# A gated merge of two token mixers: its steps in written order, four weights fetched early, three output tiles in program order

## The chip, the cores and the metric

The kernel runs on one core of a Trainium2 chip. The metric is device microseconds (us) of one execution, the median of several runs. Within the core, TensorE (PE) multiplies, VectorE (DVE) and ScalarE (ACT) work elementwise, GpSimd (POOL) does small sums and issues some transfers, and SyncE (SP) issues most transfers. Every engine works through its own queue in order.

## The reference, cut to what matters

One layer of an encoder block on x of 512 rows by 1024 columns, all in float32:

```
x = x + 1/2 * SwiGLU(RMSNorm(x))                       # FFN 1
h = RMSNorm(x); p = h @ W_in                           # all projections of the mixers and gates
y_A = RWKV7(...) @ rwkv_proj                           # 8 heads x 64
y_B = ForgettingAttention(...) @ fox_proj              # 8 heads x 64
x = x + (sigmoid(g_A) * y_A + sigmoid(g_B) * y_B) @ w_out      # the merge
x = x + 1/2 * SwiGLU(RMSNorm(x))                       # FFN 2
out = RMSNorm(x)

# the end of RWKV7, per head of 64 columns:
y = (y - mean(y)) * rsqrt(var(y) + eps) * lnx_g + lnx_b
y = (y + bonus) * (sigmoid(g_lo) @ g_up)
```

## The kernel before

Activations lie transposed: a tile is 128 columns of the model (partitions) by the 512 rows of x. A product in float32 is made of three fast matmuls: every operand is split into a high part and a low part (`hi` is a rounded copy made on ScalarE, `lo` the difference made on VectorE), and hi x hi, hi x lo and lo x hi are summed in one PSUM bank (`mm3`).

A weight tile goes this way: SP issues its transfer into a `raw` buffer (three of them, in rotation, so a transfer waits until VectorE has made the low half of the tile three before), ScalarE makes `whi`, VectorE `wlo` (two pairs, in rotation, so a cast waits until TensorE has read the pair two before). `own=` gives a split weight a buffer of its own instead: with a number n, the tiles in which the normed inputs `xh{n}` and `xl{n}` stand at other times.

The stage of the change is the merge. Before it stand the delta rule of RWKV-7 (in chunks), the attention, and the last gates (`early`, PSUM tile `pgt`). The merge itself has these parts:

- `proj` with `fox_proj`: eight output tiles (m = 0 to 7, called fox 0 to fox 7 here) of twelve matmuls each into the bank `ppj`; the gate step on VectorE (`G<-G,ppj`) empties the bank.
- The norm of RWKV's output for four head pairs p: `center` times y gives the centred y in the bank `yc` (two matmuls, y being split into `parts`); ScalarE squares it; the square is split (`shi`, `slo`) and summed over the head by two matmuls into the bank `pg`; ScalarE takes logarithm and exponential (`Tall`); VectorE multiplies, scales and adds the bonus; one product in full float32 with `gup` (written as two TensorE records per matmul) gives the gate, VectorE multiplies by it, and the result is split into `ya`.
- `proj` with `rwkv_proj`: eight tiles of twelve matmuls (rwkv 0 to 7), which need all four `ya`; VectorE adds the two mixers, and the sum is split (`mh`, `ml`). Three of the gates' tanhs (`late_tanh`) stand on ScalarE behind the last `ya`, after a table load.
- `w_out`: eight tiles of 24 matmuls into the bank `pw`; VectorE adds the residual, and the norm for FFN 2 begins.

The program is written in one order, and a scheduler of the framework places the instructions on each engine's queue by a simulated time. Two tools override it: `tc.issue_after(x)`, which places what is under it behind x, and `tc.keep_in_program_order(x)`, by which x keeps its place in the written order of its engine. In the merge of the kernel before, only table loads are kept; matmuls of the norm, of fox_proj, of rwkv_proj and of w_out are placed by the scheduler, which lets tiles run into each other.

Of the kernel before, what the change touches and what calls it, by code (L numbers as in the profile page):

```python
# [12 lines left out]
AF = mybir.ActivationFunctionType  # L13
ALU = mybir.AluOpType
# [4 lines left out]
P = 128  # L19
T = 512  # L20
D = 1024
KD = D // P
# [3 lines left out]
NP = DA // P  # L26
# [9 lines left out]
PAR_W0, PAR_A0, PAR_KK, PAR_KA, PAR_RK, PAR_LG, PAR_LB = 38, 42, 46, 50, 54, 58, 62  # L36
# [15 lines left out]
def kernel(  # L52
# [6 lines left out]
    nc = tc.nc  # L59
    dve, act, pool, pe = nc.vector, nc.scalar, nc.gpsimd, nc.tensor  # L60
# [37 lines left out]
    epsl = cp.tile([P, 1], F32, name="epsl")  # L98
# [4 lines left out]
    sel = cp.tile([P, 8], F32, name="sel")  # L103


    def load_raw(aps, kt, n, raw=None):
        if raw is None:
            raw = wp.tile([P, kt, n], F32, tag="raw", name="raw", bufs=3)
        for c0, src in aps:
            nc.sync.dma_start(raw[:, :, c0:c0 + src.shape[1]],  # L110
                              src.rearrange("(k p) c -> p k c", p=P))
        return raw

    def split_w(raw, kt, n, eng=None, own=None):
        if own is None:
            hi = wp.tile([P, kt, n], F32R, tag="whi", name="whi", bufs=2)
            lo = wp.tile([P, kt, n], F32R, tag="wlo", name="wlo", bufs=2)
        elif isinstance(own, int):
            hi, lo = [xp.tile([P, kt, n], F32R, tag=f"x{i}{own}", name=f"own{i}{own}") for i in "hl"]
        else:  # L120
            hi, lo = own
        act.copy(hi[:], raw[:])  # L122
        (eng or dve).tensor_tensor(lo[:], raw[:], hi[:].bitcast(F32), op=ALU.subtract)  # L123
        return hi, lo

    def load_w(aps, kt, n, eng=None, own=None):
        return split_w(load_raw(aps, kt, n), kt, n, eng, own)

    def mm3(ps, whi, wlo, xhi, xlo, first, last):
        pe.matmul(ps, whi, xhi, start=first, stop=False)  # L130
        pe.matmul(ps, whi, xlo, start=False, stop=False)  # L131
        return pe.matmul(ps, wlo, xhi, start=False, stop=last)  # L132

    def ln_act(out, in_, **kw):
        pre = act.preload_act_table_set("natural_log_exp_and_others")
# [4 lines left out]
    def halved(src):  # L140
        hi, lo = tmp("shi", dt=F32R), tmp("slo", dt=F32R)
        act.copy(hi[:], src)
        dve.tensor_tensor(lo[:], src, hi[:].bitcast(F32), op=ALU.subtract)
        return hi, lo

    def summed(ps, mat, parts):
        for i, part in enumerate(parts):
            pe.matmul(ps, mat[:], part[:], start=i == 0, stop=i == 1)

    def exact(ps, mat, src):  # L150
        summed(ps, mat, halved(src))

    def split(dst_hi, dst_lo, src, hi_eng="act"):
        cast = act.copy(dst_hi, src) if hi_eng == "act" else dve.tensor_copy(dst_hi, src)
        dve.tensor_tensor(dst_lo, src, dst_hi.bitcast(F32), op=ALU.subtract)
        return cast
# [77 lines left out]
    def pc(i):  # L234
        return par[:, i:i + 1]
# [11 lines left out]
    with tc.tile_pool(name="x0", bufs=1) as x0:  # L247
        xin = [x0.tile([P, NB, D // 4], F32, name=f"xin{g}") for g in range(4)]
        own = [[x0.tile([P, KD, P], F32R, name=f"first{i}{w}") for i in "hl"] for w in range(2)]
        wraw = [x0.tile([P, KD, P], F32, name=f"wraw{w}") for w in range(2)]  # L250
        first = []
# [5 lines left out]
        for c in range(KD):  # L257
            ps = bank("xtp", pr)
# [79 lines left out]
    def ffn(nrm, w1, w3, w2, nxt, during=(), first=None, final=None):  # L338
        with tc.tile_pool(name="hp", bufs=1) as hp:
# [86 lines left out]
    with ExitStack() as mx:  # L426
# [7 lines left out]
        def duo(tag, name, dt=F32):  # L434
            return sp.tile([P, 2, T], dt, name=name, tag=tag)
# [33 lines left out]
        lg = tmp("lg")  # L469
# [44 lines left out]
        vs = [V4[:, p] for p in range(NP)]  # L514
# [141 lines left out]
        for t in range(C - 1):  # L656
            n, m = t + 1, C - 1 - t
# [177 lines left out]
        for p in range(NP):  # L835
# [16 lines left out]
            for i, bl in enumerate(((0, 1), (2,), (3,))):  # L852
                at = {b: sum(c + 1 for c in bl[:j]) * P for j, b in enumerate(bl)}
                w = sum(b + 1 for b in bl) * P
                lps, trs = [], []
                for q in range(2):
                    lp = pf.tile([P, T], F32, tag="b", name="lp")
                    lps.append(lp)
                    for b in bl:
                        n, bs = (b + 1) * P, slice(b * P, (b + 1) * P)  # L860
# [4 lines left out]
                for q in range(2):  # L865
                    pt, mx = pts[:, q], mx_[q]
                    for b in bl:
                        n, mb = (b + 1) * P, mx[:, b:b + 1]
# [29 lines left out]
                    early(3 * p - 2 + i)  # L898
            yb.append(qp)

        def proj(m, wt, y):
            wh, wl = load_w([(0, wt[0][:, m * P:(m + 1) * P])], NP, P)
            ps = bank("ppj")
            for k in range(NP):
                mm3(ps[:], wh[:, k, :], wl[:, k, :], y[k][0], y[k][1], k == 0, k == NP - 1)
            return ps


        def halves(tiles):
# [19 lines left out]
        for p in range(NP):  # L929
            y = vs[p]  # L930
            yc = bank("yc", pr)
            for i in range(2):
                pe.matmul(yc[:], center[:], parts[p][i], start=i == 0, stop=i == 1)
            sq = gslot[8 + p % 2]
            act.activation(sq, yc[:], AF.Square)
            ps = bank("pg", pf)
            exact(ps[:], bonesr, sq)
            rn = tslot[p]
            with tc.issue_after(logs.ins):
                act.activation(rn, ps[:], AF.Ln, bias=epsl[:, 0:1], scale=1.0 / 64)  # L940
                act.activation(rn, rn, AF.Exp, scale=-0.5)
            dve.tensor_tensor(y, yc[:], rn, op=ALU.mult)
            dve.scalar_tensor_tensor(y, y, pc(PAR_LG + p), bons[p], op0=ALU.mult, op1=ALU.add)
            ps = bank("pg", pf)
            pe.matmul(ps[:], gup[0:96, p * P:(p + 1) * P], lg[0:96, :], start=True, stop=True)
            dve.tensor_tensor(y, y, ps[:], op=ALU.mult)
            parted = split(*ya[p], y)
# [7 lines left out]
        for m in range(KD):  # L955
            g = gslot[m]
            nc.gpsimd.dma_start(g, gsave[KD + m])
            ps = proj(m, fox_proj, ybs)
            dve.scalar_tensor_tensor(g, g, 1.0, ps[:], op0=ALU.add, op1=ALU.mult)
        fctx.close()  # L960


# [6 lines left out]
        def late_tanh(m, behind):  # L969
            if m < NP + 3:  # L970
                with tc.issue_after(behind.ins):
                    act.activation(slot[m], slot[m], AF.Tanh, scale=0.5)
# [7 lines left out]
        ms = []  # L980
# [90 lines left out]
```

## Time and profile before

| | us |
|---|---|
| median of 3 runs | 1191.12 (1190.68 to 1191.21) |
| profiled execution | 1190.24 |
| its span in the profile | 1188.5 |
| TensorE busy | 1169.2 (98%) |
| VectorE busy | 662.1 (56%) |
| ScalarE busy | 457.1 (38%) |
| first fox_proj matmul to first matmul of FFN 2 | 715.85 to 815.51 |

The profiled execution is one run; its span is 1.7 us shorter than its own time, and its time is 0.9 us under the median. In the rows of the profile "L130" is a line of the kernel, "out<-in" names tiles, "x2" counts instructions, and in brackets stands the idle time of the engine just before, and what ended it.

### The profile page before, as it was taken

What the parts mean: (1) busy time and instruction counts of PE and PEld (TensorE: products, weight loads), DVE (VectorE), ACT (ScalarE), POOL (GpSimd) and SP (SyncE); (2) the same over time, 40 slices, a digit from 0 to 9 for tenths busy, and PEclk for the clock granted to TensorE, in tenths of its full rate; (3) what the DMA queues carried; (4) which work ended last, traced back from release to release, by engine and by line L of the source; (5) the groups of instructions that cost most, each with busy time, mean ns of one, the idle gap of its engine ahead of it and who ended that gap; (6) DMA issues with size and microseconds to landing.
All of it is one profiled execution on the core that took longest, in us unless ns stands there. A gap on an engine that the chain in (4) does not pass through costs nothing.

```text
span 1188.5 us, 15870 instructions
## 1 busy us (share of the span) xinstructions
PE 1169.2 (98%) x6334; PEld 952.3 (80%) x6334; DVE 662.1 (56%) x993; ACT 457.1 (38%) x739; POOL 100.4 (8%) x144
## 2 busy tenths in 40 slices
PE   8999999999999999999999999999999999999997
PEld 7888888888887888887767777778888888888887
DVE  6555545443444888686766657866545545543242
ACT  6322222222223855346776756524222222222221
POOL 4200000001111112401000011121000000000110
PEclk9999999999999999999999999999999999999999
DMA  7333333323333433344212135633333333323331
GB/s 200 89 91 104 89 106 89 103 83 115 116 116 96 121 108 111 111 124 116 55 46 87 55 99 175 193 100 107 89 98 98 90 105 91 104 80 98 98 98 72
DMA packets 208152, 122.54 MB, mean 103 GB/s; under 512 B 9902, under 2 KB 200430, under 8 KB 208078
## 3 DMA queue, kind: packets, MB, share of 16 engines
q1 hardware_dynamic: 202078, 108.67, 31.8%
q0 software_dynamic: 3760, 12.06, 3.2%
q8 instruction: 50, 0.82, 0.3%
q10 hardware_dynamic: 2240, 0.79, 0.3%
q14 instruction: 24, 0.20, 0.1%
HBM read 110.82 MB, written 10.68 MB: 102 GB/s over the span
## 4 chain that ended last, share of the span: by engine, by line
PE 95%; DVE 3%; ACT 1%; DMA 1%; issue 0%; POOL 0%; SPq 0%; DVEq 0%; POOLq 0%
PE pd L131 7%; PE pd L130 7%; PE pd L132 7%; PE pa L132 7%; PE pa L131 7%; PE pb L131 7%; PE pb L132 7%; PE pa L130 7%; PE pb L130 7%; PE pgt L130 3%; PE pgt L132 2%; PE pgt L131 2%; PE pk L130 2%; PE pk L132 2%; PE pk L131 2%; PE pw L132 1%
## 5 line engine op out<-in xcount | busy, mean ns | idle before, releaser
L122 ACT CAST whi<-raw 128x1024 fp32r<-128x1024 f32 (+2 forms) x197 | 196.4, 998 | 605.9 <-PE pa L131 175.5
L123 DVE TENSOR_TENSOR wlo<-raw,whi 128x1024 fp32r<-128x1024 f32 (+2 forms) x197 | 227.5, 1155 | 129.1 <-ACT whi L122 129.0
L132 PE MATMUL pa<-xh,wlo 128*128 128x512 f32 x344 | 133.9, 389 | 0.0
L131 PE MATMUL pa<-xl,whi 128*128 128x512 f32 x344 | 133.8, 389 | 0.0
L132 PE MATMUL pb<-xh,wlo 128*128 128x512 f32 x344 | 133.8, 389 | 0.0
L130 PE MATMUL pa<-xh,whi 128*128 128x512 f32 x344 | 133.8, 389 | 0.0
L130 PE MATMUL pb<-xh,whi 128*128 128x512 f32 x344 | 133.8, 389 | 0.0
L131 PE MATMUL pb<-xl,whi 128*128 128x512 f32 x344 | 133.8, 389 | 0.0
L132 PE MATMUL pd<-hh,wlo 128*128 128x512 f32 x330 | 129.0, 391 | 0.0
L131 PE MATMUL pd<-hl,whi 128*128 128x512 f32 x330 | 128.5, 389 | 0.0
L130 PE MATMUL pd<-hh,whi 128*128 128x512 f32 x330 | 128.4, 389 | 0.0
L350 DVE TENSOR_TENSOR fb<-pb,rstd 128x512 f32<-128x512 f32 x43 | 29.7, 691 | 137.2 <-PE pb L132 137.2
L130 PEld LDWEIGHTS pa<-xh,whi 128*128 128x128 f32 x344 | 64.6, 188 | 13.5
L132 PEld LDWEIGHTS pb<-xh,wlo 128*128 128x128 f32 x344 | 64.6, 188 | 13.4
L131 PEld LDWEIGHTS pb<-xl,whi 128*128 128x128 f32 x344 | 64.6, 188 | 13.5
L132 PEld LDWEIGHTS pa<-xh,wlo 128*128 128x128 f32 x344 | 64.5, 188 | 13.5
L131 PEld LDWEIGHTS pa<-xl,whi 128*128 128x128 f32 x344 | 64.6, 188 | 13.4
L130 PEld LDWEIGHTS pb<-xh,whi 128*128 128x128 f32 x344 | 64.5, 188 | 13.4
L131 PEld LDWEIGHTS pd<-hl,whi 128*128 128x128 f32 x330 | 61.9, 188 | 12.9
L132 PEld LDWEIGHTS pd<-hh,wlo 128*128 128x128 f32 x330 | 62.0, 188 | 12.7
L130 PEld LDWEIGHTS pd<-hh,whi 128*128 128x128 f32 x330 | 62.0, 188 | 12.7
L346 DVE TENSOR_TENSOR fa<-pa,rstd 128x512 f32<-128x512 f32 x43 | 29.7, 691 | 68.5 <-PE pa L132 68.4
(397 smaller groups left out, 1964.5 us busy)
## 6 DMA issues: line engine op xcount, KB each, us to landing
raw<-in_ffn_w_dram SPq DMA_DIRECT2D x116, 512.0 KB
raw<-in_w_in_dram SPq DMA_DIRECT2D x40, 512.0 KB
raw<-in_ffn_w_dram SPq DMA_DIRECT2D x15, 384.0 KB
raw<-in_w_out_dram SPq DMA_DIRECT2D x8, 512.0 KB
gsave<-gs SPq DMA_DIRECT2D x9, 256.0 KB
xin<-in_x_dram SPq DMA_DIRECT2D x4, 512.0 KB
xsave<-xT POOLq DMA_DIRECT2D x8, 256.0 KB, 2.3
G<-gsave POOLq DMA_DIRECT2D x8, 256.0 KB, 3.8
```

The lines of the kernel that those rows point to most:

```text
L122: act.copy(hi[:], raw[:])
L123: (eng or dve).tensor_tensor(lo[:], raw[:], hi[:].bitcast(F32), op=ALU.subtract)
L130: pe.matmul(ps, whi, xhi, start=first, stop=False)
L131: pe.matmul(ps, whi, xlo, start=False, stop=False)
L132: return pe.matmul(ps, wlo, xhi, start=False, stop=last)
L346: dve.tensor_tensor(a[:], pa[:], nrm.rstd[:], op=ALU.mult)
L350: dve.tensor_tensor(b[:], pb[:], nrm.rstd[:], op=ALU.mult)
```

## The change

The products of fox_proj and the steps of the norm are written in an explicit order (`fox`, `centred`, `squared`, `summing`, `normed_y`), and their matmuls keep it on TensorE. The first four rwkv_proj weights (`ahead_of`, m = 0 to 3) are fetched and split between fox_proj's tiles 4 to 7, each into a buffer of its own. The transfers of the fox weights from m = 4 on and of all rwkv weights keep their written order on SP. In w_out the matmuls of the first three tiles keep the written order. The number of instructions of each kind and their shapes stay the same.

```diff
-    def load_raw(aps, kt, n, raw=None):
+    def load_raw(aps, kt, n, raw=None, keep=False):
...
+            if keep:
+                tc.keep_in_program_order(got)
...
-    def mm3(ps, whi, wlo, xhi, xlo, first, last):
...
+    def mm3(ps, whi, wlo, xhi, xlo, first, last, keep=False):
+        for n, (w, x_) in enumerate(((whi, xhi), (whi, xlo), (wlo, xhi))):
+            mm = pe.matmul(ps, w, x_, start=first and n == 0, stop=last and n == 2)
+            if keep:
+                tc.keep_in_program_order(mm)
+        return mm
...
-        def proj(m, wt, y):
-            wh, wl = load_w([(0, wt[0][:, m * P:(m + 1) * P])], NP, P)
+        def proj_w(m, wt, own=None):
+            return load_w([(0, wt[0][:, m * P:(m + 1) * P])], NP, P, own=own, keep=wt is rwkv_proj or m > 3)
+
+        def proj(w, y):
+            wh, wl = w
             ps = bank("ppj")
             for k in range(NP):
-                mm3(ps[:], wh[:, k, :], wl[:, k, :], y[k][0], y[k][1], k == 0, k == NP - 1)
+                for n, (a, b) in enumerate(((wh, 0), (wh, 1), (wl, 0))):
+                    keep(pe.matmul(ps[:], a[:, k, :], y[k][b], start=k == 0 and n == 0, stop=k == NP - 1 and n == 2))
             return ps
...
+        fox(0)
+        for p in range(NP):
+            centred(p, pr if p < 3 else pf)
+        squared(0)
+        squared(1)
+        fox(1)
+        squared(2)
+        squared(3)
+        fox(2)
+        summing(0)
+        summing(1)
+        fox(3)
+        summing(2)
+        summing(3)
+        rw = []
+
+        def ahead_of(m):
+            rw.append(proj_w(m, rwkv_proj, own=m))
+
+        fox(4)
+        normed_y(0)
+        normed_y(1)
+        ahead_of(0)
+        fox(5)
+        normed_y(2)
+        parted = normed_y(3)
+        ahead_of(1)
+        fox(6)
+        ahead_of(2)
+        fox(7)
+        ahead_of(3)
...
-            ps = proj(m, rwkv_proj, ya)
+            ps = proj(rw[m] if m < 4 else proj_w(m, rwkv_proj), ya)
...
-                mm3(ps[:], wh[:, k, :], wl[:, k, :], ms[k][0], ms[k][1], k == 0, k == KD - 1)
+                mm3(ps[:], wh[:, k, :], wl[:, k, :], ms[k][0], ms[k][1], k == 0, k == KD - 1, m < 3)
```

The new functions hold the steps that the loop over p held before; `normed_y(p)` has the three VectorE steps, the product with `gup` and the split into `ya`, `summing(p)` the two matmuls into `pg` with logarithm and exponential, and the bank `yc` of the fourth pair comes from the pool `pf`, so that all four stand at once.

How the queues move, at three places. On SP, the transfers of the merge from the fifth fox weight on (the weights `raw`, and the last saved gates `gsave`), before:

```order
L921 DMA G_2718<-lgsave 96x512
L924 DMA G_2719<-bsave 128x512
L924 DMA G_2720<-bsave 128x512
L689 DMA gsave<-gs 128x512
L110 DMA raw<-in_fox_proj_dram 128x4x128
L689 DMA gsave<-gs 128x512
L110 DMA raw<-in_fox_proj_dram 128x4x128 x3
L110 DMA raw<-in_rwkv_proj_dram 128x4x128 x8
L110 DMA raw<-in_w_out_dram 128x8x128 x8
```

and now:

```order
L693 DMA gsave<-gs 128x512
L110 DMA raw<-in_fox_proj_dram 128x4x128
L693 DMA gsave<-gs 128x512
L110 DMA raw<-in_rwkv_proj_dram 128x4x128
L110 DMA raw<-in_fox_proj_dram 128x4x128
L110 DMA raw<-in_rwkv_proj_dram 128x4x128
L110 DMA raw<-in_fox_proj_dram 128x4x128
L110 DMA raw<-in_rwkv_proj_dram 128x4x128
L110 DMA raw<-in_fox_proj_dram 128x4x128
L110 DMA raw<-in_rwkv_proj_dram 128x4x128 x5
L110 DMA raw<-in_w_out_dram 128x8x128 x8
```

Fox weights 5, 6 and 7 each stand behind an rwkv weight now.

On ScalarE, from the norm of the last head pairs to the table load and the tanhs (`ga`); in the first list the `whi` are those of fox 7, rwkv 0 and 1 and, behind the tanhs, rwkv 2 and 3:

```order
L142 CAST shi_6248<-G20_2717 128x512
L122 CAST whi_6494<-raw_6492 128x512
L154 CAST ya2_6159<-V4_2881 128x512
L122 CAST whi_6518<-raw_6516 128x512
L940 ACTIVATE Tall_2729<-pg_6247,epsl_99 128x512
L941 ACTIVATE Tall_2729<-Tall_2729 128x512
L154 CAST ya3_6160<-V4_2881 128x512
L972 ACT_TABLE_LOAD
L972 ACTIVATE ga0_6449<-ga0_6449 128x512 x2
L972 ACTIVATE ga1_6450<-ga1_6450 128x512
L122 CAST whi_6542<-raw_6540 128x512
L122 CAST whi_6566<-raw_6564 128x512
```

and now, with the casts of rwkv weights 2 and 3 (`ownh2`, `ownh3`) and of fox 7 (`whi_6447`) ahead:

```order
L972 ACTIVATE Tall_2729<-Tall_2729 128x512 x2
L124 CAST whi_6420<-raw_6418 128x512
L124 CAST ownh2_6440<-raw_6438 128x512
L158 CAST ya0_6157<-V4_2881 128x512
L124 CAST whi_6447<-raw_6445 128x512
L158 CAST ya1_6158<-V4_2881 128x512
L124 CAST ownh3_6467<-raw_6465 128x512
L158 CAST ya2_6159<-V4_2881 128x512
L158 CAST ya3_6160<-V4_2881 128x512
L1026 ACT_TABLE_LOAD
L1026 ACTIVATE ga0_6473<-ga0_6473 128x512 x2
L1026 ACTIVATE ga1_6474<-ga1_6474 128x512
```

The norm's logarithms stand further ahead, and all four early weights are cast before the table load.

On TensorE, the end of the first two output tiles of w_out (the banks `pw_6686` and `pw_6724`) and the start of the third and fourth (`pw_6763`, `pw_6802`), before:

```order
L132 MATMUL pw_6724<-mh30_6490,wlo_6721 128x512
L130 MATMUL pw_6686<-mh31_6491,whi_6682 128x512
L130 MATMUL pw_6724<-mh31_6491,whi_6720 128x512
L131 MATMUL pw_6724<-ml1_6487,whi_6720 128x512
L132 MATMUL pw_6724<-mh31_6491,wlo_6721 128x512
L131 MATMUL pw_6686<-ml1_6487,whi_6682 128x512
L132 MATMUL pw_6686<-mh31_6491,wlo_6683 128x512
L130 MATMUL pw_6724<-mh31_6491,whi_6720 128x512
L131 MATMUL pw_6724<-ml1_6487,whi_6720 128x512
L132 MATMUL pw_6724<-mh31_6491,wlo_6721 128x512
L130 MATMUL pw_6763<-mh20_6488,whi_6759 128x512
```

and now, the end of the first and the start of the second:

```order
L133 MATMUL pw_6686<-mh31_6515,whi_6682 128x512
L133 MATMUL pw_6686<-ml1_6511,whi_6682 128x512
L133 MATMUL pw_6686<-mh31_6515,wlo_6683 128x512
L133 MATMUL pw_6724<-mh20_6512,whi_6720 128x512
L133 MATMUL pw_6724<-ml0_6510,whi_6720 128x512
L133 MATMUL pw_6724<-mh20_6512,wlo_6721 128x512
```

The first tile's last three matmuls stood among the second tile's last ones; now the first tile ends before the second begins, and the second before the third. On all engines the order outside the merge and w_out's first tiles is as before.

More of the change, by code (lines that the diff above doesn't have):

```diff
@@ L109, in load_raw @@
         for c0, src in aps:
-            nc.sync.dma_start(raw[:, :, c0:c0 + src.shape[1]],
-                              src.rearrange("(k p) c -> p k c", p=P))
+            got = nc.sync.dma_start(raw[:, :, c0:c0 + src.shape[1]],
+                                    src.rearrange("(k p) c -> p k c", p=P))
+            if keep:
+                tc.keep_in_program_order(got)
         return raw
@@ L124, in split_w, with load_w @@
         return hi, lo
-    def load_w(aps, kt, n, eng=None, own=None):
-        return split_w(load_raw(aps, kt, n), kt, n, eng, own)
-    def mm3(ps, whi, wlo, xhi, xlo, first, last):
-        pe.matmul(ps, whi, xhi, start=first, stop=False)
-        pe.matmul(ps, whi, xlo, start=False, stop=False)
-        return pe.matmul(ps, wlo, xhi, start=False, stop=last)
+    def load_w(aps, kt, n, eng=None, own=None, keep=False):
+        return split_w(load_raw(aps, kt, n, keep=keep), kt, n, eng, own)
+    def mm3(ps, whi, wlo, xhi, xlo, first, last, keep=False):
[4 more added lines that the diff above has]
+        return mm
     def ln_act(out, in_, **kw):
@@ L899 @@
             yb.append(qp)
-        def proj(m, wt, y):
-            wh, wl = load_w([(0, wt[0][:, m * P:(m + 1) * P])], NP, P)
+        keep = tc.keep_in_program_order
+        def proj_w(m, wt, own=None):
+            return load_w([(0, wt[0][:, m * P:(m + 1) * P])], NP, P, own=own, keep=wt is rwkv_proj or m > 3)
+        def proj(w, y):
+            wh, wl = w
             ps = bank("ppj")
             for k in range(NP):
-                mm3(ps[:], wh[:, k, :], wl[:, k, :], y[k][0], y[k][1], k == 0, k == NP - 1)
+                for n, (a, b) in enumerate(((wh, 0), (wh, 1), (wl, 0))):
+                    keep(pe.matmul(ps[:], a[:, k, :], y[k][b], start=k == 0 and n == 0, stop=k == NP - 1 and n == 2))
             return ps
@@ L928 @@
             split(*parts[p], vs[p])
[L929 to L947, printed above, removed]
         ybs = []
@@ L954, with fox, centred, squared @@
             ybs.append((o[:], l[:]))
-        for m in range(KD):
+        def fox(m):
             g = gslot[m]
             nc.gpsimd.dma_start(g, gsave[KD + m])
-            ps = proj(m, fox_proj, ybs)
+            ps = proj(proj_w(m, fox_proj), ybs)
             dve.scalar_tensor_tensor(g, g, 1.0, ps[:], op0=ALU.add, op1=ALU.mult)
+        ycs, sums, roots = [], [], []
+        def centred(p, pool_):
+            yc = bank("yc", pool_)
+            for i in range(2):
+                keep(pe.matmul(yc[:], center[:], parts[p][i], start=i == 0, stop=i == 1))
+            ycs.append(yc)
+        def squared(p):
+            sq = gslot[8 + p % 2]
+            act.activation(sq, ycs[p][:], AF.Square)
+            sums.append(halved(sq))
+        def summing(p):
+            ps = bank("pg", pf)
+            for i in range(2):
+                keep(pe.matmul(ps[:], bonesr[:], sums[p][i][:], start=i == 0, stop=i == 1))
+            rn = tslot[p]
+            with tc.issue_after(logs.ins):
+                act.activation(rn, ps[:], AF.Ln, bias=epsl[:, 0:1], scale=1.0 / 64)
+                act.activation(rn, rn, AF.Exp, scale=-0.5)
+        def normed_y(p):
+            y = vs[p]
+            dve.tensor_tensor(y, ycs[p][:], tslot[p], op=ALU.mult)
+            dve.scalar_tensor_tensor(y, y, pc(PAR_LG + p), bons[p], op0=ALU.mult, op1=ALU.add)
+            ps = bank("pg", pf)
+            keep(pe.matmul(ps[:], gup[0:96, p * P:(p + 1) * P], lg[0:96, :], start=True, stop=True))
+            dve.tensor_tensor(y, y, ps[:], op=ALU.mult)
+            return split(*ya[p], y)
+        fox(0)
[27 more added lines that the diff above has]
+        ahead_of(3)
         fctx.close()
```

## The prediction, made before the changed kernel ran

> **What bounds the kernel now.** I read the page's head first, then the chain of work that ended last, then who waited for whom between 700 and 820 us (the merge and its neighbours), then the timelines of TensorE, ScalarE, VectorE and the SP queue there.
>
> ```profile
> span 1188.5 us, 15870 instructions
> PE 1169.2 (98%) x6334; PEld 952.3 (80%) x6334; DVE 662.1 (56%) x993; ACT 457.1 (38%) x739; POOL 100.4 (8%) x144
> PE 95%; DVE 3%; ACT 1%; DMA 1%; issue 0%; POOL 0%; SPq 0%; DVEq 0%; POOLq 0%
> ...
> PE ppj L130 <- ACT whi L122: 1.6, 1, 1.6
> PE ppj L130 <- ACT ya L154: 0.7, 1, 0.7
> PE pw L130 <- ACT whi L122: 0.5, 2, 0.3
> PE pw L132 <- DVE wlo L123: 0.3, 1, 0.3
> ```
>
> TensorE is the bound: 95% of the chain. No matmul is removed by the change, so it can only win the time in which TensorE stands still or waits, and lose by new waits. The last four lines (waiter, released by: us in all, times, longest) are the waits of the merge. They are small and understate the loss, so I measured it on the timeline (start, us busy, then the instruction):
>
> ```profile
> 715.85 0.50 PE L130 MATMUL ppj<-yh,whi 128*128 128x512 f32 x1 [0.20 <-DVE gs L680]
> ...
> 722.84 0.40 PE L130 MATMUL ppj<-yh,whi 128*128 128x512 f32 x1
> ...
> 728.07 0.39 PE L132 MATMUL ppj<-yh,wlo 128*128 128x512 f32 x1
> ...
> 748.88 0.39 PE L132 MATMUL ppj<-ya,wlo 128*128 128x512 f32 x1
> 750.02 0.73 PE L130 MATMUL ppj<-ya,whi 128*128 128x512 f32 x2 [0.75 <-ACT ya L154]
> ...
> 751.54 0.40 PE L132 MATMUL ppj<-ya,wlo 128*128 128x512 f32 x1
> 753.51 0.50 PE L130 MATMUL ppj<-ya,whi 128*128 128x512 f32 x1 [1.57 <-ACT whi L122]
> ...
> 780.95 0.39 PE L132 MATMUL pw<-mh,wlo 128*128 128x512 f32 x1
> 781.62 0.50 PE L130 MATMUL pw<-mh,whi 128*128 128x512 f32 x1 [0.28 <-ACT whi L122]
> ...
> 783.65 0.50 PE L132 MATMUL pw<-mh,wlo 128*128 128x512 f32 x1 [0.35 <-DVE wlo L123]
> ...
> 815.51 0.39 PE L130 MATMUL pa<-xh,whi 128*128 128x512 f32 x1
> ```
>
> From 722.84 to 728.07 two tiles run without a gap: 23 steps in 5.23 us, 0.2274 us each. That is the dense pitch. The gaps are: 748.88 to 750.02 (1.14, so 0.9 lost), 751.54 to 753.51 (1.97, 1.7 lost), and five steps from 780.95 to 783.65 (2.70, 1.6 lost). The chain of work, in order of time, says why the first two are there:
>
> ```profile
> 744.07 0.86 PE pg L945 x2
> ...
> 745.65 0.70 ACT Tall L940
> ...
> 747.04 0.70 DVE V L942
> ...
> 749.98 1.28 ACT L972
> ...
> 751.81 1.13 ACT ga L972 x2
> 752.95 0.52 ACT whi L122
> ```
>
> The fourth head pair's norm (root on ScalarE, three VectorE steps) runs so late that rwkv_proj's first tiles use up everything else; behind it ScalarE loads a table and takes three tanhs before the cast of the third rwkv_proj weight. The gap at 781 has another cause: w_out's tiles 0 and 1 end together, so neither frees its split weights early enough for tile 2.
>
> **The floor and the sum.** From 715.85 (first fox_proj matmul) to 815.51 (first matmul of FFN 2) are 99.66 us. The work in it is 192 matmuls of the two projections, 192 of w_out, 8 of centring, 8 of the sums: 400 x 0.2274 = 90.96; and four products with gup in full float32 at 0.86 each (the row at 744.07) = 3.44. Floor 94.40, so 5.26 us are lost. This is the most the change can win. All that stands behind 815.51 keeps its order on every engine, so what is won is kept to the end.
>
> **The change, step by step on the trace's clock.** TensorE's new order, if nothing waits: fox 0 at 715.85, eight centrings 718.7, fox 1 720.5, fox 2 723.3, sums 0 and 1 726.0, fox 3 726.9, sums 2 and 3 729.6, fox 4 730.6, two gup products 733.3, fox 5 735.0, two gup products 737.7, fox 6 739.5, fox 7 742.2, rwkv 0 744.9, w_out 0 766.8, FFN 2 810.3. I checked each step against the engines that feed it, with these rows:
>
> ```profile
> 722.34 1.09 ACT L935 ACTIVATE G<-yc 128x512 f32<-128x512 f32 x2
> 728.27 0.62 ACT L122 CAST whi<-raw 128x512 fp32r<-128x512 f32 x1 [2.10 <-PE ppj L131]
> 729.82 1.26 ACT L940 ACTIVATE Tall<-pg,epsl 128x512 f32<-128x512 f32 x2 [0.41 <-PE pg L148]
> 717.06 0.69 DVE L155 TENSOR_TENSOR yqa<-V,yqa 128x512 fp32r<-128x512 f32 x1
> 717.67 0.68 DVE L155 TENSOR_TENSOR ykb<-V,ykb 128x512 fp32r<-128x512 f32 x1
> 732.84 0.74 DVE L943 SCALAR_TENSOR_TENSOR V<-V,par,G 128x512 f32<-128x512 f32 x1
> ...
> 717.45 0.38 SPq L110 DMA_DIRECT2D raw<-in_fox_proj_dram  x1
> 721.80 1.77 SPq L110 DMA_DIRECT2D raw<-in_fox_proj_dram  x2
> 735.48 3.89 SPq L110 DMA_DIRECT2D raw<-in_rwkv_proj_dram  x2
> SPq L110 <- DMA raw<-in_fox_proj_dram: 1.7, 1, 1.7
> ...
> 737.00:738.00 1.00, 1.00 (x6) 0.82 (x5) 0.92 (x2) 1.00 (x3) 0.00 (x0) 1.00 0.60 180
> 738.00:739.00 1.00, 1.00 (x6) 0.81 (x5) 1.00 (x3) 1.00 (x3) 0.00 (x0) 1.00 0.00 0
> ```
>
> ScalarE spends some 0.5 us from start to start of a cast or square and 0.6 of a logarithm; VectorE starts a 128x512 step each 0.61 us (717.06, 717.67), each 0.66 with the scalar form. A transfer of 256 KB among others: the one issued at 717.45 had landed when SP's wait of 1.7 us ended, 723.6 + 1.7 = 725.3, so 7.8 us. On a quiet queue: the one issued at 735.48 was through by 738 (in the one-microsecond windows the last number, GB/s, falls from 180 to 0), at most 2.5 us. I take 2.4 for the early weights issued after 727, since they meet the quiet half of the merge, and keep 7.8 as the other end.
>
> - *rwkv weight 0* goes to SP's place of fox weight 5, 721.80. Its cast on ScalarE stands before the logarithms of sums 0 and 1 and before the cast for sum 3. Fox weight 5, from that place, was there at 728.27 at the latest, and not before 725.3, as one queue serves in order. ScalarE reaches the cast at 727.0; I take no delay. Then logarithms 727.6 and 728.2, cast 728.8, VectorE's low half of square 3 from 729.4 to 730.1. TensorE wants it at 730.3: 0.2 to spare.
> - *rwkv weight 1* may be issued when fox weight 4 is split (727.5), lands near 730.0, and its cast at 730.5 stands before fox 5's and before logarithms 2 and 3 (done 732.9). The gup products need the banks that these free, at 733.3 and 734.2. Spare: 0.4 to 1.
> - *Fox weights 5, 6 and 7* each move behind an rwkv weight on SP: issued at 725.4, 728.8 and 734.2 where it was 721.8 to 727.1. Their casts come at 731.0, 734.0 and 737.7, more than 2.4 later each; hidden.
> - *rwkv weights 2 and 3* (issued 733.8 and 737.5) are cast at 736.2 and 739.9, ahead of ya 0 and ya 2, whose inputs VectorE has ready only at 736.8 and 742.9. Hidden, if 2.4 holds.
> - *VectorE* has 28 steps from the low half of square 3 to the low half of ya 3: 23 x 0.60 + 4 x 0.66 = 16.4, so the last ends at 729.4 + 16.4 + 0.7 = 746.5. rwkv 0 wants it at 744.9 + 10 x 0.2274 = 747.2; it wants the bank that fox 6's gate step frees (744.7) at 744.9. The spare 0.2 to 0.7 is thin: VectorE is full there.
> - *The table load and the three tanhs* now end near 747.8 and the casts of rwkv weights 4 and 5 near 749, wanted from 755.8 on. This cover of four tiles (10.9 us) is what removes the 2.6 us at 749 to 753.5.
> - *The own buffers* reuse the normed input's tiles, last read by the gates' matmuls before 715; no wait.
> - *w_out tiles 0 to 2 in order*: tile 0 ends at 772.2, weight 2 is split by 775, wanted at 777.7. The 1.6 us at 781 go. New: tile 0 wants ml 7 at 771.8, VectorE has it at 771.5.
> - *POOL* keeps its order. The final gain's and xsave's reads start when fox 7 ends, 745 where it was 743.9; first wanted at 772.5.
>
> Sum: the loss of 5.26 falls to what the thin places give. I estimate 0.5 for them (three with 0.2 to 0.3 to spare, between 0 and 1.2). Gain 4.8. The profiled execution took 1190.24 us (span 1188.5 and 1.7 around it), 0.9 under the median 1191.12; it becomes 1185.4, and the median 1186.3.
>
> [...]
>
> **Rivals.**
> 1. *The first early weight comes late.* Between 725 and 729 the core moves 347, 316, 220 and 277 GB/s:
>
> ```profile
> 725.00:726.00 1.00, 1.00 (x6) 0.84 (x5) 0.48 (x2) 0.80 (x2) 0.00 (x0) 1.00 1.16 347
> 728.00:729.00 1.00, 1.00 (x7) 0.64 (x5) 0.51 (x1) 0.73 (x2) 0.00 (x0) 1.00 0.80 277
> ```
>
> If SP's queue and POOL's share this evenly, the weight and the gate write ahead of it, 0.5 MB, take over 3 us from 725.3; the row at 728.27 caps it there. The cast is then 1.2 late, sum 3 waits 1.0, all behind shifts: 1187.3.
> 2. *VectorE becomes the bound.* If its 28 steps take their full 0.69 instead of 0.60 apart (they do where each waits for ScalarE), the chain ends 2.4 later and rwkv 0 stands 1.9: 1188.2.
> 3. *Thin places and w_out give back most.* The 1.6 at w_out stays in another form and the merge's tight places cost 1.2: gain 2.5 to 2, 1188.9. For it: three places with under 0.3 to spare; against: weight 2 has 2.7.
> 4. *Slower: the early weights take as long as the one issued at 717.45,* 7.8 us each. ScalarE is in order, so the cast of weight 1 holds fox 5's cast and logarithms 2 and 3 until 735.4 (gup products 3.7 late), weight 2, issued only after fox 5's split near 738, holds ya 0 and fox 7's cast until 746; fox 7, planned at 742.2, then starts near 750: 7.7 lost, 1194.0. It decides from about 6.5 us a transfer. Against it: 2.5 at 735.48, and a DMA share that was 0.18 in 730 to 740.
>
> ```profile
> 730.00:735.00 5.00, 5.00 (x24) 4.12 (x23) 3.95 (x7) 2.75 (x5) 0.00 (x0) 1.00 0.18 55
> 735.00:740.00 5.00, 5.00 (x22) 3.78 (x21) 4.56 (x8) 3.59 (x7) 0.00 (x0) 1.00 0.18 52
> ```
>
> **Numbers.** Forecast 0.55 (its own range 1185.6 to 1187.1), first rival 0.12, second 0.12, third 0.13, fourth 0.08. The likeliest: 1186.3. With 0.2% (2.4 us, about what a measurement of this kernel can tell) the border of faster is 1188.7: forecast, first rival and two thirds of the second, with a little of the third, 0.78; same 0.14; slower 0.08. The range goes from the floor (1191.1 - 5.3 - 0.5 for the scatter of the runs) to the third rival, 1185.3 to 1189.0; it leaves out the fourth and half of the third.
>
> **What would show it.** Right: no wait of a ppj matmul above 0.5 us, rwkv 0 within 29 to 29.6 us of fox 0, FFN 2 within 94.4 to 95.6. First rival: the wait of pg for the low half of the fourth square near 730. Second: ppj waiting for ya or for the gate step of fox 6. Fourth: ScalarE idle before the own casts until a DMA. The forecast is wrong if one of the own casts sits more than 1 us behind its transfer.

## The result, and the profile after

| | before | after |
|---|---|---|
| median | 1190.90 us (4 runs, 1189.08 to 1191.21) | 1184.99 us (4 runs, 1184.30 to 1185.54) |
| ratio of the runs | | 0.9952, 95% interval 0.9939 to 0.9964 |
| profiled execution, its span | 1190.24, 1188.5 | 1184.30, 1182.6 |
| first fox_proj matmul to FFN 2 (the merge) | 99.66 | 94.59 |
| FFN 2 to the end of the span | 373.0 | 373.0 |

The kernel became 4.3 to 7.3 us faster. The forecast was 1186.3 us with a range of 1185.3 to 1189.0; the time lies 0.3 us below the range. Head of the page after, and the share of the chain by engine:

```profile
span 1182.6 us, 15856 instructions
PE 1166.8 (99%) x6334; PEld 953.1 (81%) x6334; DVE 663.8 (56%) x993; ACT 457.0 (39%) x739; POOL 100.7 (9%) x144
PE 95%; DVE 3%; DMA 1%; ACT 1%; issue 0%; SPq 0%; POOL 0%; DVEq 0%; POOLq 0%
```

The counts of busy instructions are those of before; the 14 fewer in the head (15856 for 15870) are of kinds that the page does not count as busy.

TensorE's timeline through the merge (start, us busy, then the instruction; brackets would show a wait):

```profile
714.99 0.50 PE L915 MATMUL ppj<-yh,whi 128*128 128x512 f32 x1 [0.20 <-DVE gs L684]
717.85 0.63 PE L957 MATMUL yc<-yqa,center 128*128 128x512 f32 x2
...
733.80 0.80 PE L915 MATMUL ppj<-yh,whi 128*128 128x512 f32 x1
736.95 1.88 PE L979 MATMUL pg<-G 96*128 96x512 f32 x4
...
744.13 0.63 PE L915 MATMUL ppj<-ya,ownh 128*128 128x512 f32 x2
...
765.91 0.39 PE L133 MATMUL pw<-mh,whi 128*128 128x512 f32 x1
...
809.58 0.39 PE L133 MATMUL pa<-xh,whi 128*128 128x512 f32 x1
```

The only wait is the one in the first row, which the kernel before has too. rwkv 0 starts 29.14 us after fox 0 and FFN 2 94.59 us after it, 0.19 above the floor of 94.40. The loss of 5.26 us fell to 0.19: the merge gives 5.07 us. Behind it nothing changed. Ahead of it, in code that the change does not touch, fox 0 starts at 714.99 instead of 715.85: the first pair of profiles shows 0.86 us more than the merge gave. Where that is from had to be found.

The casts of the early weights on ScalarE (brackets: idle time before, and what ended it), and the last low half on VectorE:

```profile
726.20 0.62 ACT L124 CAST ownh<-raw 128x512 fp32r<-128x512 f32 x1
730.10 0.62 ACT L124 CAST ownh<-raw 128x512 fp32r<-128x512 f32 x1 [0.57 <-DMA raw<-in_rwkv_proj_dram]
734.44 0.62 ACT L124 CAST ownh<-raw 128x512 fp32r<-128x512 f32 x1 [0.49 <-DMA raw<-in_rwkv_proj_dram]
739.26 0.62 ACT L124 CAST ownh<-raw 128x512 fp32r<-128x512 f32 x1 [1.20 <-DMA raw<-in_rwkv_proj_dram]
...
720.95 0.38 SPq L110 DMA_DIRECT2D raw<-in_rwkv_proj_dram  x1
726.70 0.37 SPq L110 DMA_DIRECT2D raw<-in_rwkv_proj_dram  x1
731.63 0.37 SPq L110 DMA_DIRECT2D raw<-in_rwkv_proj_dram  x1
736.55 1.57 SPq L110 DMA_DIRECT2D raw<-in_rwkv_proj_dram  x2
...
744.96 0.69 DVE L159 TENSOR_TENSOR ya<-V,ya 128x512 fp32r<-128x512 f32 x1
```

Weight 0 was there when ScalarE came to it. Weights 1 to 3 took 3.4, 2.8 and 2.7 us from issue to cast (730.10 - 726.70 and so on), and ScalarE waited up to 1.2 us for them. TensorE waited for none of these casts.

### The profile page after: what moved, and what is told of

Same layout as the page of the kernel before. It is cut to its first block, busy times and chain, and to the rows that moved or that the text cites. A ratio compares the mean times of both kernels' runs of the same rounds, so it can differ in the third digit from the quotient of the medians.

```text
span 1182.6 us, 15856 instructions
## 1 busy us (share of the span) xinstructions
PE 1166.8 (99%) x6334; PEld 953.1 (81%) x6334; DVE 663.8 (56%) x993; ACT 457.0 (39%) x739; POOL 100.7 (9%) x144
## 4 chain that ended last, share of the span: by engine, by line
PE 95%; DVE 3%; DMA 1%; ACT 1%; issue 0%; SPq 0%; POOL 0%; DVEq 0%; POOLq 0%
PE pd L133 20%; PE pa L133 20%; PE pb L133 20%; PE pgt L133 7%; PE pk L133 6%; PE ppj L915 4%; PE pw L133 4%; PE pq L133 3%; PE pv L133 2%; PE f L133 1%; PE pl L133 1%; PE sps L799 1%; PE lp L895 1%; PE gp L617 1%; PE lp L884 1%; DMA xin<-in_x_dram 1%
## 5 line engine op out<-in xcount | busy, mean ns | idle before, releaser
L124 ACT CAST whi<-raw 128x1024 fp32r<-128x1024 f32 (+2 forms) x193 | 193.9, 1005 | 599.2 <-PE pa L133 175.3
L125 DVE TENSOR_TENSOR wlo<-raw,whi 128x1024 fp32r<-128x1024 f32 (+2 forms) x193 | 224.9, 1165 | 130.6 <-ACT whi L124 130.6
```

## The experiments

The runs were made in three groups. The kernel before, run beside them, had medians of 1190.56 (23 runs), 1190.75 (24) and 1190.43 (15); ratios are against those. The theory that they test: each of the three gaps of the merge is removed by a part of the change that can be told apart, and the rest is scatter. The merge's length (fox 0 to FFN 2 in the profile) proved the sharper measure: 99.66 and 99.71 in two profiles of the kernel before, 94.59, 94.61 and 94.60 in three of the changed one.

**The same two kernels again** (no edit).

> The kernel before, once more, to see how its opening scatters. Theory A (the 0.86 us that the changed kernel won ahead of the merge is scatter of the opening transfers): time 1189 to 1191.3; the second batch of the opening transposes starts somewhere between 8.5 and 9.6 us in this profile, and fox 0 and all that follows move with it by the same amount, the merge (fox 0 to FFN 2) again 99.4 to 99.9 us. Rival (the changed kernel's opening is systematically earlier, for instance because its program is shorter by 14 instructions): the second batch starts at 9.5 to 9.6 again, and the time is within 0.3 of 1190.5.

> The changed kernel, once more. Theory A (scatter): time 1184.3 to 1187, the second batch of the opening transposes somewhere between 8.5 and 9.6 us, the merge 94.5 to 94.8 us whatever the opening does; ratio to the kernel before 0.994 to 0.997. Rival (systematic): the second batch at 8.5 to 8.7 again, time 1184.3 to 1185.5.

> The changed kernel a third time, on the chip of the two runs beside it, for the scatter. Theory (the merge gives 5.07 us every time, all else is where the windows of half clock fall): merge 94.5 to 94.7 us; the profile shows one or two windows of 3.41 us at a granted clock of 0.5 in the first 16 us or at 610 us, each behind a window in which TensorE was busy less than some 0.53 of the time; time 1183.9 to 1187. Rival (the changed kernel wins something ahead of the merge as well): time of every run under 1185.5.

Measured: before 1189.51 (11 runs, 1189.02 to 1191.36; ratio 0.9995, 0.9986 to 1.0004); after 1185.25 (5 runs; 0.9957, 0.9944 to 0.9969) and 1185.50 (5 runs, up to 1187.15; 0.9959, 0.9947 to 0.9972). Over its 14 runs the changed kernel has a median of 1185.3. The opening's second batch of transposes started at 8.59 in the repeated kernel before, as in the changed one, so its opening is not systematically earlier. (In the two repeats of the changed kernel it started at 8.27 and 8.44, a little before the 8.5 that I had expected at the earliest.) But the merge of that run started later, at 716.24: against the first profile it had lost 1.5 us between 611 and 615. The windows view shows it (stretch, its length, busy us of TensorE, PEld, VectorE, ScalarE, POOL, then the granted clock, DMA share and GB/s). The kernel before, repeated:

```profile
607.90:611.30 3.40, 1.46 (x13) 0.88 (x14) 3.24 (x8) 2.31 (x6) 0.00 (x0) 1.00 0.00 0
611.30:614.70 3.40, 3.40 (x16) 2.25 (x14) 2.74 (x8) 1.55 (x5) 0.00 (x0) 0.50 0.00 0
```

And the kernel before in its first profile, at the same code, in its opening, and over the longest gap of its merge:

```profile
607.77:611.18 3.41, 2.23 (x26) 1.54 (x18) 3.25 (x7) 2.94 (x6) 0.00 (x0) 1.00 0.00 0
611.18:614.60 3.42, 2.65 (x21) 1.86 (x19) 3.29 (x8) 2.12 (x7) 0.00 (x0) 1.00 0.00 0
7.03:10.44 3.41, 0.87 (x9) 0.90 (x9) 2.20 (x3) 2.84 (x5) 0.00 (x0) 1.00 1.11 322
10.44:13.86 3.42, 3.42 (x12) 2.75 (x11) 2.99 (x5) 2.46 (x4) 1.50 (x1) 0.50 1.13 324
...
750.00:753.40 3.40, 1.92 (x6) 0.97 (x6) 1.97 (x3) 3.39 (x6) 0.11 (x1) 1.00 1.06 382
```

Where TensorE was busy for 1.46 of 3.40 us (0.43), the next 3.4 us ran at half clock; where 2.23 of 3.41 (0.65), at full clock. The waits at 610 are the same in both (1.17 and 0.77 us in the repeat, 1.18 and 0.77 in the first profile), and why the clock fell in one alone is not shown; where I laid the stretches that full clock followed is my choice. In the other rows shown in this document, about 3.4 us near half clock stood behind busy shares of 0.26 (before, 7.03 to 10.44) and 0.33 (after, 5.50 to 8.90; early_only, 749.40 to 752.80), and full clock behind 0.56 (before, 750.00 to 753.40; 1.00 in 753.50 to 757.00), 0.73 and 0.77 (fill). The "some 0.53" in two of the expectations is an estimate of mine from such shares, here between 0.43 and 0.56. By estimate 3.4 us at half clock cost 3.4 x (1 - 0.2274/0.43) = 1.6 us where TensorE has no waits, 0.2274 being the dense pitch and 0.43 the pitch in the half clock of early_only (rows below). The times agree that such windows are a large part of the scatter: of the 62 runs of the kernel before that stood beside the others, the 20 with a mean granted clock of 0.997 or more took 1188.65 to 1190.33 us, the 42 with less 1190.16 to 1194.07.

The 0.86 us of the first pair are not these windows, since both openings have one (0.50 in 10.44 to 13.86 before, in 8.90 to 12.30 after). They are the start of the second batch of transposes, shown here with the first product of FFN 1, in the kernel before and then in the changed one:

```profile
9.57 1.12 PE L260 MATMUL xtp<-ident,xin 128*128 128x128 f32 x8 [2.55 <-DVE firstl L123]
24.80 0.39 PE L130 MATMUL pa<-xh,whi 128*128 128x512 f32 x1
...
8.59 1.69 PE L264 MATMUL xtp<-ident,xin 128*128 128x128 f32 x8 [2.27 <-DMA xin<-in_x_dram]
24.02 0.39 PE L133 MATMUL pa<-xh,whi 128*128 128x512 f32 x1
```

The batch started 0.98 earlier, and 0.78 of that was left at FFN 1. In the eleven other profiles the batch started at 8.27 to 9.03, in the repeated kernel before at 8.59, so 9.57 is the odd one; what held it there stays open. Theory A, scatter of the opening, stands; the rival, that all runs of the third group would stay under 1185.5, fell (1185.65 and 1187.15).

**One part alone, or one part left out.** wout_only adds to the kernel before only

```
-                mm3(ps[:], wh[:, k, :], wl[:, k, :], ms[k][0], ms[k][1], k == 0, k == KD - 1)
+                mm3(ps[:], wh[:, k, :], wl[:, k, :], ms[k][0], ms[k][1], k == 0, k == KD - 1, m < 3)
```

and no_wout takes only this line back from the changed kernel.

> The kernel before with only the last part of the change: w_out's first three tiles in written order. Theory (the five steps from 780.95 to 783.65 lose 1.6 us because tiles 0 and 1 end together, and nothing else holds tile 2): the gap goes, the merge takes 98.0 to 98.2 us, time 1.4 to 1.7 us under the kernel before (about 1189.2 against 1190.9); the gaps at 748.9 and 751.5 stay. Rival (what is won there is given back by the ordered start of tile 0, which needs the last low half of the merged sum earlier): gain under 0.5 us, with a wait of the first pw matmuls for DVE ml.

> The changed kernel without the written order in w_out. Theory (the parts add up): tiles 0 and 1 end together again and tile 2 waits for its split weight: 1.4 to 1.7 us over the changed kernel, about 1186.6, merge 96.0 to 96.3 us. Rival (with the rwkv casts gone early, ScalarE and VectorE are ahead at w_out, and tile 2's weight is ready anyway): within 0.4 us of the changed kernel, no wait of pw for whi or wlo.

Measured: wout_only's merge 98.13 (1.55 gained), time 1189.68 (0.9994, 0.9986 to 1.0003), 0.9 under the median beside it where I had 1.4 to 1.7; no_wout's 96.20 (1.60 lost), 1186.51 (0.9972, 0.9961 to 0.9983). In no_wout the waits of the kernel before stand again in tile 2, and nowhere else in the merge:

```profile
777.85 0.50 PE L133 MATMUL pw<-mh,whi 128*128 128x512 f32 x1 [0.28 <-ACT whi L124]
778.80 0.51 PE L133 MATMUL pw<-mh,whi 128*128 128x512 f32 x1 [0.22 <-ACT whi L124]
779.88 0.50 PE L133 MATMUL pw<-mh,wlo 128*128 128x512 f32 x1 [0.35 <-DVE wlo L125]
```

This part is worth 1.6 us with or without the rest. By time alone, with an interval of 2 us, wout_only could not have shown it; the profile could.

early_only adds to the kernel before only the early weights; no_early takes only them from the changed kernel:

```
early_only, in the loop over fox_proj's tiles:
+            if m > 3:
+                rw.append(load_w([(0, rwkv_proj[0][:, (m - 4) * P:(m - 3) * P])], NP, P, own=m - 4))
...
-            ps = proj(m, rwkv_proj, ya)
+            ps = proj(m, rwkv_proj, ya, rw[m] if m < 4 else None)
no_early:
-        ahead_of(0)
-        ahead_of(1)
-        ahead_of(2)
-        ahead_of(3)
-            ps = proj(rw[m] if m < 4 else proj_w(m, rwkv_proj), ya)
+            ps = proj(proj_w(m, rwkv_proj), ya)
```

> The kernel before with only the early weights: the first four rwkv weights are fetched between the fox weights into buffers of their own, nothing keeps a written order on TensorE. Theory (the gap of 1.7 us at 751.54 to 753.51 is the cast of rwkv weight 2 standing behind the table load and three tanhs; the other two gaps have other causes): that gap goes, the wait for ya at 749 (0.9) and the five slow steps in w_out (1.6) stay; merge 97.8 to 98.2 us against 99.7, time 1.5 to 1.9 us under the kernel before. Rival (without the written order the early casts only push the norm's steps on ScalarE and VectorE back, and the wait for ya grows by what the cast saves): merge 99 us or more, the wait of ppj for ya above 1.5 us.

> The changed kernel without early weights: the written order of projections, norm and three w_out tiles stays, the rwkv weights go through the rotating buffers as before. Theory (the cover of four weights is what hides the table load and the tanhs): the cast of rwkv weight 0 stands behind the last ya, the table load and three tanhs, near 746.5 to 747 on the changed kernel's clock, its low half 0.6 later; rwkv 0, wanted at 744.1, waits 2.5 to 4.5 us: merge 97.1 to 99.1 us, time 1187.7 to 1190. Rival (the written order alone brings the norm forward enough that the casts are no longer held): merge under 95.6 us, no wait of ppj for whi above 0.8.

Measured: no_early's merge 97.16, time 1188.27 (0.9977, 0.9966 to 0.9988), as the theory has it in sum: 2.57 more than with early weights, though rwkv 0 starts only 1.0 later (I had put 2.5 to 4.5 there) and the rest is lost at later weights. early_only went the rival's way: merge 100.86, time 1192.16 (1.0012, 1.0002 to 1.0021), slower than before. Its ScalarE, then its TensorE:

```profile
739.45 0.62 ACT L122 CAST ownh<-raw 128x512 fp32r<-128x512 f32 x1 [3.81 <-DMA raw<-in_rwkv_proj_dram]
739.98 0.68 ACT L940 ACTIVATE Tall<-pg,epsl 128x512 f32<-128x512 f32 x1
...
751.91 0.62 ACT L154 CAST ya<-V 128x512 fp32r<-128x512 f32 x1 [2.34 <-DVE V L946]
...
752.58 1.20 PE L130 MATMUL ppj<-ya,ownh 128*128 128x512 f32 x2 [2.29 <-ACT ya L154]
753.58 0.63 PE L131 MATMUL ppj<-ya,ownh 128*128 128x512 f32 x1
754.00 0.63 PE L132 MATMUL ppj<-ya,ownl 128*128 128x512 f32 x1
```

ScalarE stood 3.8 us at the cast of an early weight, with a logarithm of the norm behind it; counted from fox 0, the cast of the fourth ya came 1.8 us later than before (751.91 - 716.58 against 749.35 - 715.85), and TensorE waited 2.29 us for it instead of 0.75. In the 3.40 us with that wait TensorE was busy for 0.33 (1.11 of 3.40), and the next 3.40 ran near half clock (0.52), 0.43 us a step:

```profile
749.40:752.80 3.40, 1.11 (x5) 0.60 (x4) 2.37 (x4) 1.04 (x3) 0.55 (x1) 0.97 1.03 380
752.80:756.20 3.40, 3.40 (x8) 2.15 (x9) 1.75 (x4) 2.69 (x4) 0.00 (x0) 0.52 1.06 349
```

So the wait cost its length and, by the estimate above, 1.6 us more; without the halved clock the merge would be about 99.3, a gain of 0.4 and not 1.7. The parts, by the merge's length:

| kernel | w_out's order | written order | early weights | merge, us |
|---|---|---|---|---|
| before | | | | 99.66, 99.71 |
| wout_only | x | | | 98.13 |
| early_only | | | x | 100.86 |
| no_early | x | x | | 97.16 |
| no_wout | | x | x | 96.20 |
| after | x | x | x | 94.59, 94.61, 94.60 |

Added one behind the other, w_out's order gives 1.55, the written order 0.97, the early weights 2.57: 5.1 together. The early weights have that worth only behind the written order. The written order alone, without the other two parts, was not run.

**How much the early weights and VectorE can bear.** slow2 and slow3 fetch each early weight two and three times into the same buffer (the last copy counts); dve4 adds four steps to the last chain of the norm, which change no value:

```
slow2, slow3:
-        for c0, src in aps:
+        for c0, src in aps * times:        # times = 2 or 3 for the early weights
dve4, in normed_y ahead of the split:
+            for _ in range(4 if p == 3 else 0):
+                dve.tensor_scalar(y, y, 1.0, None, op0=ALU.mult)
```

> The changed kernel with each of the four early weights fetched three times into the same buffer, one transfer behind the other; all else stays, but the scheduler sets the early casts some places later on ScalarE (the first behind the first logarithm of the norm). With 2.7 to 3.4 us for one transfer as the changed kernel's trace shows, an early weight then takes 8 to 10 us. The prediction's fourth rival (decides from 6.5 us a transfer; 7.7 us lost at 7.8): merge 99 to 104 us, with ScalarE idle before the own casts until a transfer and fox 7 or a gup product waiting. Rival (the buffers' rotation and the later places leave slack for it, and late weights cost only their own tile): merge under 97 us.

> The changed kernel with each early weight fetched twice into the same buffer, one transfer behind the other, so about 5 to 5.6 us each. With 7.5 us each the merge lost 7.7 us beside what the halved clock took; the prediction has it decide at 6.5 us (4.8 lost). Theory (a ramp from about 4.3 us a transfer, some 2.2 us for each us more): merge 96 to 97.5 us. Rival (a step: below 6 us the rotation of the buffers hides the whole): merge under 95.2 us.

> The changed kernel with four more VectorE steps (a multiplication by one in place, 128x512) in the norm's last chain, ahead of the fourth ya. Theory (VectorE is full from 729 to 746 and its spare at rwkv 0 is 0.75 us, by the changed kernel's trace: low half of the fourth ya done at 745.65, wanted at 746.4): four steps of 0.6 to 0.7 us, less the spare, make rwkv 0 wait for ya 1.6 to 2.3 us; merge 96.2 to 96.9 us. Rival (VectorE has pauses that take them up): merge under 95 us.

slow3: merge 104.77 (I had 99 to 104), time 1195.34 (1.0039, 1.0023 to 1.0054), slower than before. Its casts of early weights, with the waits for transfers, and the fox tile behind them:

```profile
740.41 0.62 ACT L124 CAST ownh<-raw 128x512 fp32r<-128x512 f32 x1 [4.84 <-DMA raw<-in_rwkv_proj_dram]
747.89 0.62 ACT L124 CAST ownh<-raw 128x512 fp32r<-128x512 f32 x1 [4.86 <-DMA raw<-in_rwkv_proj_dram]
748.88 0.62 ACT L124 CAST whi<-raw 128x512 fp32r<-128x512 f32 x1 [0.36 <-DMA raw<-in_fox_proj_dram]
...
749.55 0.80 PE L916 MATMUL ppj<-yh,whi 128*128 128x512 f32 x1 [4.17 <-ACT whi L124]
...
751.00:754.40 3.40, 3.40 (x9) 2.62 (x8) 0.64 (x2) 2.51 (x4) 0.00 (x0) 0.51 0.41 118
```

The casts stand 7.5 us apart (747.89 - 740.41); from its first issue to its cast a weight took 9.3 to 11.5 us. The merge lost 10.2 us; from 749.55 to 754.4 TensorE ran at half clock (0.50 in 747.60 to 751.00, 0.51 in 751.00 to 754.40), which is 2.3 of it by the same estimate. The other 7.9 are close to the fourth rival's 7.7 and come by its road, an early cast in front of fox 7's cast, but at longer transfers than its 7.8. slow2, with its casts 4.5 to 5.5 us apart and 5.4 to 10.3 from first issue to cast: merge 97.40 (2.8 lost), time 1188.04 (0.9981, 0.9970 to 0.9992), in the range that was expected. So the loss is no step but grows with the transfers. How much longer the changed kernel's own transfers, 2.7 to 3.4 from issue to cast, could be without a loss is not shown: in slow2 and slow3 the fox weights wait on SP behind the added transfers too, and the early casts stand some places later on ScalarE.

dve4: merge 97.51 (2.9 lost; I had 1.6 to 2.3), time 1189.04 (0.9986, 0.9976 to 0.9996). VectorE's timeline, then TensorE's:

```profile
746.57 0.42 DVE L982 TENSOR_SCALAR V<-V 128x512 f32<-128x512 f32 x1
746.91 0.68 DVE L950 SCALAR_TENSOR_TENSOR G<-G,ppj 128x512 f32<-128x512 f32 x1
747.50 0.88 DVE L982 TENSOR_SCALAR V<-V 128x512 f32<-128x512 f32 x2
748.30 0.68 DVE L125 TENSOR_TENSOR wlo<-raw,whi 128x512 fp32r<-128x512 f32 x1
748.90 0.46 DVE L982 TENSOR_SCALAR V<-V 128x512 f32<-128x512 f32 x1
750.04 0.69 DVE L159 TENSOR_TENSOR ya<-V,ya 128x512 fp32r<-128x512 f32 x1 [0.68 <-ACT ya L158]
...
750.06 0.50 PE L915 MATMUL ppj<-ya,ownh 128*128 128x512 f32 x1 [1.62 <-ACT ya L158]
```

Against the changed kernel (744.96, with fox 0 1.64 earlier) the last low half starts 3.44 later: the four steps are shorter than the others (0.42 to 0.46 for 0.68), but a weight's low half slipped in between them, and the cast on ScalarE now waits for the chain. 3.44 later cost 2.9: a spare of 0.5 us, where the changed kernel's rows give 0.75 (done at 745.65, wanted at 744.13 + 10 x 0.2274 = 746.4).

**Filling the first wait**, to test what halves the clock, and as a candidate for a faster kernel: the changed kernel with

```
+            if c == 1:
+                with tc.issue_after(turned.ins):      # the eighth transpose of x
+                    for _ in range(6):
+                        pe.matmul(warm[:, 0:P], ones_[:], ones_[:], start=True, stop=True)
```

> The changed kernel with six more warm-up products (128x128, result not used) on TensorE in its first wait, behind the first eight transposes of x, where the changed kernel stood for 2.0 to 2.3 us. Theory (a window of 3.41 us in which TensorE is busy under some 0.53 is followed by one at half clock, and the waits of the opening cause the ones near 8 to 14 us): no window of half clock in the opening, or a later one; the first product of FFN 1 behind the opening starts at 22.5 to 23.3 us instead of 23.5 to 24.0, time 0.5 to 1.5 us under the changed kernel. Rival (the half clock there has nothing to do with the wait, or the products delay the transposes by as much): half clock as before, time within 0.5 us of the changed kernel or above it.

Measured: 1185.81 (5 runs; 0.9966, 0.9952 to 0.9979), no better than the changed kernel. The changed kernel's opening, then the filled one's:

```profile
5.50:8.90 3.40, 1.13 (x11) 0.93 (x10) 1.05 (x1) 2.12 (x4) 0.00 (x0) 1.00 1.07 309
8.90:12.30 3.40, 3.40 (x13) 2.95 (x12) 3.20 (x6) 3.09 (x5) 0.38 (x1) 0.50 1.11 340
```

```profile
5.50:8.90 3.40, 2.63 (x20) 2.44 (x18) 1.63 (x3) 2.64 (x4) 0.00 (x0) 1.00 1.06 307
8.90:12.30 3.40, 2.49 (x14) 1.96 (x15) 1.40 (x3) 2.18 (x4) 0.46 (x1) 1.00 1.10 338
```

The half clock is gone from this opening (1.00 from 0 to 18 us), as the theory has it. One profile does not show that the wait was the cause, since the repeated kernel before had no half clock in its opening either; but the runs agree, with a mean granted clock of 0.997 to 0.999 in the five with the filling and 0.996 in all five of the changed kernel beside them. The time was not won. The six products made the scheduler place the opening's instructions anew: the first product of FFN 1 started at 21.15, before the 22.5 to 23.3 that I had expected, but products of the opening still stood behind it, and fox 0 started at 715.59, no earlier than in the changed kernel. And the merge took 95.46, for a reason that the prediction had named:

```profile
727.80 0.62 ACT L124 CAST ownh<-raw 128x512 fp32r<-128x512 f32 x1 [0.87 <-DMA raw<-in_rwkv_proj_dram]
...
730.88 0.50 PE L972 MATMUL pg<-slo,bonesr 128*128 128x512 f32 x1 [0.23 <-DVE slo L147]
```

Weight 0, issued at 721.55, arrived 6.2 us later instead of within 5.2 (720.95 to 726.20), ScalarE waited 0.87, and everything up to the fourth square's low half shifted: 0.86 lost. This is the first rival, though no run here shows the shares of the two queues. Why the weight was slower in this run stays open.

## Why the prediction was right or wrong

- *The bound and the loss in the merge, 5.26 us over a floor of 94.40:* right. The changed merge takes 94.59 to 94.61 in three profiles, so nearly all of the loss was there to win, and no more. The signs named for it came: no wait of a ppj matmul above 0.20, rwkv 0 29.14 behind fox 0, FFN 2 94.59.
- *The three gaps and their causes:* right in size. w_out's order gave 1.55 for 1.6; the early weights gave 2.57 for the 2.6 at 749 to 753.5; the written order gave the other 0.97. What the prediction left out is that the early weights need the written order: alone they lost.
- *The transfers, 2.4 us each:* too short, 2.7 to 3.4. It cost nothing that shows: ScalarE waited 0.5 to 1.2 us at these casts, and no product waited behind them. How near it was to costing something, no run shows.
- *The thin places, 0.5 us between 0 and 1.2:* this term was mis-sized. It measured 0.19. The low half of the fourth square ended at 729.21 and was wanted at 729.53; the last low half of ya had 0.5 to 0.75, where I had 0.2 to 0.7. Places with 0.2 to 0.3 to spare do not each lose something on average: here they held, or, as in fill, broke by 0.86 at once.
- *The time before, and the lower end of the range:* this is the step that failed. The sum was set on the median of three runs, 1191.12, as if the profiled run lay 0.9 under the usual. Longer series gave 1190.43 to 1190.75, 0.4 to 0.7 lower, and the eleven runs of the repeated kernel 1189.51, 1.6 lower; single runs lie between 1188.65 and 1194.07. I allowed 0.5 for scatter under the floor; a median of three or four runs moves by as much on both sides of the comparison. From 1190.6, the mean of all 77 runs of the kernel before, with 5.26 less 0.19 won, the sum is 1185.5; over 14 runs the changed kernel has 1185.3, and eight of them lie under the lower end of my range, so the range stood too high and was not only missed by chance. That the four runs of the result fell 0.3 lower still is scatter. Of the 1.3 us by which the forecast was too high, 0.5 is this base and 0.3 the thin places; the other 0.5 I can't tell from scatter. A large part of the scatter, the windows of half clock, stands in the granted clock of the opening (0.50 in 10.44 to 13.86), which I had not looked at.
- *Rivals:* the first did not occur in the changed kernel but did in fill, at 0.86 for the 1.0 it named; no run shows the even shares in its sum, only the 6.2 us from the issue of weight 0 to its cast. The second and third did not occur. The fourth's price is near that of slow3 (7.9 without the halved clock, for 7.7), but at 9.3 to 11.5 us from issue to cast, not 7.8. Its turning point near 6.5 is not settled: slow2, with 5.4 to 10.3 us, still kept 2.3 of the 5.1 won, slow3 none.

## What to carry to other kernels

Measure a small change in the stretch of the trace that it touches: the merge repeated to 0.05 us where the whole time scattered by 3 to 5, and it told parts of 1 us apart. Early fetches into buffers of their own won 2.57 us behind the written order and lost 1.2 without it (early_only, 100.86 for 99.66), where ScalarE stood 3.8 us at such a cast with a step of the norm behind it, so fix the order first. And when a forecast stands on a median of few runs, widen its range by that median's own scatter.

## What the hardware showed that I had not expected

TensorE's granted clock fell to half for about 3.4 us in places where TensorE had stood waiting: to 0.50 behind busy shares of 0.26 (before, 7.03 to 10.44), 0.33 (after, 5.50 to 8.90) and 0.43 (the repeated kernel before, 607.90 to 611.30), and to 0.52 behind 0.33 (early_only, 749.40 to 752.80). In slow3 it stayed there for twice as long, 0.50 in 747.60 to 751.00 and 0.51 in 751.00 to 754.40. In early_only the one wait was of 2.29 us; in the repeated kernel before there were two, of 1.17 and 0.77. Nearly the same pair of waits in the first profile of that kernel (1.18 and 0.77) was followed by full clock, 1.00 in 611.18 to 614.60; the repeat lost 1.5 us against it between 611 and 615. What decides between the two is not shown. I had counted a wait at its own length; in early_only, by the estimate from the pitches, it cost 1.6 us more than that.
